# A hybrid attention block: the first unit's key copies and three weight splits in another order

## The chip, the core and the metric

The kernel runs on one core of one Trainium2 chip. The engines are TensorE (PE, matmuls; its weight loads are listed as PEld), VectorE (DVE), ScalarE (ACT), GpSimd (POOL) and SyncE (SP, which here only issues transfers). Each engine has its own instruction stream and works through it in order; across engines the program waits on semaphores. The metric is the device time of one execution in microseconds (us).

## The reference

One decoder block over 16 meta tokens and 512 tokens, width 1024. Eight heads of differential attention and sixteen heads of stick-breaking attention share one input projection; each branch is gated by SiLU and projected, the branches are merged by sigmoid gates, projected out, and added to the residual under a layer norm. Cut to what matters:

```python
proj = jnp.einsum('bld,dn->bln', h, w_in[i])
q_d, k_d, v_d, g_d, q_s, k_s, v_s, g_s, m_d, m_s = jnp.split(proj, IN_OFFSETS, axis=-1)
...
outs_d.append(diff_attn_block(q_d[:, :, :, t0:t1], k_d[:, :, :, :t1], v_d[:, :, :t1],
                              q_pos, slopes, lam))
outs_s.append(stick_breaking_block(q_s[:, :, t0:t1], k_s[:, :, :t1], v_s[:, :, :t1], q_pos))
...
y_d = rms_norm(y_d, diff_subln_g[i]) * (1.0 - lam_init)
br_d = jnp.einsum('blw,wd->bld', y_d * jax.nn.silu(g_d), w_br_diff[i])
br_s = jnp.einsum('blw,wd->bld', y_s * jax.nn.silu(g_s), w_br_sb[i])
merged = jax.nn.sigmoid(m_d + b_gate[i, 0]) * br_d + jax.nn.sigmoid(m_s + b_gate[i, 1]) * br_s
y = jnp.einsum('bld,de->ble', merged, w_out[i])
```

## The kernel before

All values are fp32. A product keeps fp32's accuracy by splitting each operand into a rounded part and a remainder: ACT casts the rounded part (`hi` for weights, L185), DVE subtracts it from the original (`lo`, L190), and PE adds three products, as in L496, L497, L498 (rounded by rounded, rounded by remainder, remainder by rounded).

The work has three stretches. The first, to about 34 us, normalizes and transposes the input. The middle goes through sixteen units, eight differential heads and eight pairs of stick-breaking heads. While PE, ACT and DVE do one unit's attention, the projections of the next unit are woven into it, so that PE always has products to do. The names in one unit: `stage_q` makes the queries `A` (L618 to L621), `stage_k` and later `stage_kv` the keys (`stage_kv` by a scheme of seven products, L697); the keys are staged in `ks` (L703, L704) and stored by transfers on SP's queue into `k0` and `k1`, one tile for each head of the pair (L650, L651). Scores `sc` are matmuls of keys and queries (L761) into two PSUM banks. In a stick-breaking unit ACT reads a score bank twice (L907, L909) and DVE scans it (L913); the weights are transposed on PE (L773) and copied out; the values' products `av` (L922 to L930) are evacuated by ACT (L934, L938), and the next unit's values by ACT L750 and DVE L751. In a differential unit DVE reads the score banks (L841), ACT exponentiates (L845) and DVE combines (L849 to L851). The third stretch, after the units, has eight branch pairs (`pair`, L1055; products L1071, seven steps in three PSUM banks with copies `t` at L1076, L1078, L1080) and the output matmul (L1194), for which `split_out` splits the output weights (ACT L1136, DVE L1137) and lets SP fetch more raw weights. `merged` multiplies and adds the branches (`ss`), `rounded` and `rest` split the sums (`mh` L1116, `ml` L1119).

What sets the order: the first stretch and the third are kept on PE, DVE, ACT and POOL as they are written. There `run` steps through a generator of matmul groups, adds the time that each group states (0.35 in `pair`), and does a listed step as soon as the running time reaches the step's. The middle is written in the same manner, but its order is decided at build by the framework's scheduler, which simulates the engines and places instructions as they become ready in that simulation. So an edit ahead of the middle can change the order of instructions far behind it.

In the first unit the keys come straight from PSUM (`direct` in `stage_k`), one bank for each half of 264 columns. A key tile wants three things of a head's 64 partitions: the rounded part in one half of the partitions, the remainder beside it, and the rounded part again in the other half.

Of the kernel before, what the change touches and what calls it, by code (L numbers as in the profile page):

```python
# [42 lines left out]
LO, HI = slice(0, 64), slice(64, 128)  # L43
# [3 lines left out]
def hybrid_block_kernel(ctx: ExitStack, tc: tile.TileContext, x, meta, emb_g, emb_b, w_in, b_gate,  # L47
                        diff_lambda, subln_g, w_br_d, w_br_s, w_out, ln_g, ln_b, out):
    nc = tc.nc
    v, s, g, pe = nc.vector, nc.scalar, nc.gpsimd, nc.tensor  # L50
# [40 lines left out]
    for n, (kind, i) in enumerate(seq):  # L91
        if kind in ("BD", "BS", "wd", "ws"):
# [6 lines left out]
            o = len(loads)  # L99
# [35 lines left out]
    def fetch(most=99):  # L135

        for order, most in ((sum_loads, 1), (other_loads, most)):
            while order and most:
                l = order[0]
                src, more, tag = loads[l]  # L140
                bufs, log = rings[tag]
                if len(log) >= bufs and left[log[-bufs]] or tag not in pools:
                    break
                raw = pools[tag].tile([P, 4, P], F32, tag=tag, name=tag, bufs=bufs)
                nc.sync.dma_start(raw if l < WOUT else raw.rearrange("p a b -> p (a b)"), src)
                if more is not None:
                    second[l] = [lambda raw=raw, x=x: g.dma_start(raw, x, accum_op=ALU.add) for x in more]  # L147
                    if tag == "rawa":
                        added(l)
                    else:  # L150
                        for n in range(len(more)):
                            later.append((state["n"] + 3 + 3 * n, lambda l=l: added(l)))
                        later.sort(key=lambda x: x[0])
                raws[l] = raw
                log.append(order.pop(0))
                most -= 1
# [220 lines left out]
    def scaled(b, k, eng=s):  # L377

        o, i = hF[k][:, ds(M + P * b, P)], tps[b // 2][k // 2][:, ts(2 * (k % 2) + b % 2, P)]
        if eng is s:  # L380
            s.activation(o, i, AF.Identity, scale=cols[:, k:k + 1], bias=cols[:, 8 + k:9 + k])
        else:
            v.tensor_scalar(o, i, cols[:, k:k + 1], cols[:, 8 + k:9 + k], op0=ALU.mult, op1=ALU.add)

    def query(n, o, w, k):

        pe.matmul(pss[n][:, ds(o, w)], raw0[:, n, k, :], hF[k][:, ds(M + o, w)], start=(k == 0), stop=(k == KT - 1))  # L387
# [3 lines left out]
    def high(half, k, copy):  # L391

        copy(hTh[:, k, HALF[half]], hF[k][:, HALF[half]])
# [55 lines left out]
    def lam2():  # L449
        v.tensor_scalar(nlam, lexp[:, 1:2], lexp[:, 0:1], -LAM_INIT, op0=ALU.subtract, op1=ALU.add)  # L450

    steps = dict(a=scaled, d=lambda b, k: scaled(b, k, v), x=lambda b, k: query(0, P * b, P, k),
                 y=lambda h, k: query(1, 256 * h, 256, k), s=lambda h, k: high(h, k, s.copy),
                 h=lambda h, k: high(h, k, v.tensor_copy), l=low, N=norms, S=stat)
# [48 lines left out]
    def proj_pos(res, kind, i):  # L503
        n = take(kind, i)
        for c in range(2):
            ps = pj.tile([P, 512], F32, tag="pj", name="ps")
            if n > 4:
                prep(n + c + state["ahead"])
            for k in range(KT):
                _, wh, wl = split[n + k // 4]  # L510
                for m, (a, b) in enumerate(((wh, hTh), (wh, hTl), (wl, hTh))):
                    pe.matmul(ps[:, :H2], a[:, k % 4, :], b[:, k, ts(c, H2)], start=(k == 0 and m == 0),  # L512
                              stop=(k == KT - 1 and m == 2))
                if k < KT - 1:
                    yield 0.33
            res.append(ps)
            if c == 0:
                yield 0.33
# [43 lines left out]
    def merge_gate(c, j, t=None):  # L562
        res = []
        yield from proj_tok(res, "m" + "ds"[c], j)
        if t is None:
            t = gpool.tile([P, S], F32, tag="sg", name=f"sm{c}")
        s.activation(t, res[0], AF.Sigmoid, bias=cols[:, 16 + 8 * c + j:17 + 8 * c + j])
        sm[c, j] = t
        yield 0.64

    def run(proj, steps=()):

        steps, now = sorted(steps, key=lambda x: x[0]), 0.0
        for part in proj:
            for dt in part:
                now += dt
                while steps and steps[0][0] <= now:
                    steps.pop(0)[1]()
        for _, step in steps:
            step()  # L580


    with tc.tile_pool(name="att", bufs=1) as ap:
# [18 lines left out]
        K = [ap.tile([P, 2, L], F32R, name=f"k{c}") for c in range(2)]  # L602
# [22 lines left out]
        def stage_k(unit, kind, n, direct=False):  # L625

            pss = []
            proj = proj_pos(pss, "k" + kind, n)
            for m in range(2):
                while len(pss) == m:  # L630
                    yield next(proj, 0.33)
                o, ps = ts(m, H2), pss[m][:, :H2]
                if direct:
                    s.copy(K[0][LO, 0, o], ps[LO])
                    v.tensor_tensor(K[0][LO, 1, o], ps[LO], K[0][LO, 0, o].bitcast(F32), op=ALU.subtract)
                    s.copy(K[0][HI, 0, o], ps[LO])
                    s.copy(K[1][HI, 0, o], ps[HI])
                    v.tensor_tensor(K[1][LO, 1, o], ps[HI], K[1][HI, 0, o].bitcast(F32), op=ALU.subtract)
                    s.copy(K[1][LO, 0, o], ps[HI])  # L639
                    continue  # L640
                t = ap.tile([P, 2, H2], F32R, tag="ks", name="ks", bufs=2)
                s.copy(t[:, 0], ps)
                v.tensor_tensor(t[:, 1], ps, t[:, 0].bitcast(F32), op=ALU.subtract)
                staged.append((o, t))
# [80 lines left out]
        def values(unit, kind):  # L725

            vT = unit["vT"]
            tv = ptp.tile([P, 512], F32, tag="tp", name="tv")
            for j in range(4):
                pe.transpose(tv[:, ts(j, P)], vT[:, ts(j, P)], ident)  # L730
            tvv = tv.rearrange("p (j d) -> p j d", j=4)
            V = ap.tile([P, 1024], F32R, tag="v", name="V")
            t4 = ptp.tile([P, 512], F32, tag="tp", name="t4")[:, :P]
            pe.transpose(t4, strips(vT[:, P:], P), ident)
            if kind == "d":
                V = V.rearrange("p (c j d) -> p c j d", c=2, j=4)
                V = [V[:, c] for c in range(2)]
                s.copy(V[0][:, :3, :], tvv[:, :3, :])
                v.tensor_tensor(V[1][:, :3, :], tvv[:, :3, :], V[0][:, :3, :].bitcast(F32), op=ALU.subtract)
                s.copy(v3[:, 0:2].rearrange("p c d -> p (c d)"), tvv[:, 3, :])  # L740
                h, l = [v4[:, 2 * m:2 * m + 2].rearrange("p c d -> p (c d)") for m in range(2)]
                s.copy(h, t4)
                v.tensor_tensor(l, t4, h.bitcast(F32), op=ALU.subtract)
                unit["V"] = V
            else:

                V = V.rearrange("p (j c d) -> p j c d", j=4, c=4)[:, :3]
                for h, l, src in ((V[:, :, 0:4:3], V[:, :, 1:3], tvv[:, :3].rearrange("p j (c d) -> p j c d", c=2)),
                                  (v4[:, 0:4:3], v4[:, 1:3], t4.rearrange("p (c d) -> p c d", c=2))):
                    s.copy(h, src)  # L750
                    v.tensor_tensor(l, src, h.bitcast(F32), op=ALU.subtract)  # L751
                s.copy(v3[:, 0:3:2], tvv[:, 3].rearrange("p (c d) -> p c d", c=2))
                unit["V"] = [V[:, :, 2 * c:2 * c + 2].rearrange("p j c d -> p j (c d)") for c in range(2)]
# [206 lines left out]
        for u, (kind, n) in enumerate(UNITS):  # L960
# [7 lines left out]
            steps = pending + [(0.6, lambda unit=unit: values(unit, kind))]  # L968
# [163 lines left out]
    def split_out(c, k):  # L1132

        l = WOUT + c * KT + k
        raw = raws[l].rearrange("p a b -> p (a b)")
        s.copy(WO[c][0][:, k, :], raw)  # L1136
        v.tensor_tensor(WO[c][1][:, k, :], raw, WO[c][0][:, k, :].bitcast(F32), op=ALU.subtract)  # L1137
        left[l] -= 1
        fetch()
# [6 lines left out]
    for p in range(4):  # L1146
        steps = []
        if p == 3:
            run([merge_gate(1, 7, MS[7])], [(4.4, further)])
            WO = [[hpool.tile([P, KT, 512], F32R, tag=f"hT{x}", name=f"wo0{x}") for x in "hl"]]  # L1150
            steps = [(0.8 + 1.6 * k, lambda k=k: split_out(0, k)) for k in range(5)]
        run([pair("BS", p, G, MS[2 * p:2 * p + 2], lambda m, p=p: merged(2 * p + m))], steps)


# [29 lines left out]
    for c in range(2):  # L1184
        for t in range(NB):
            st, final = sts[t], t == NB - 1
            for o, w in [(0, 256), (256, 256)] if final and c else [(0, 512)]:
                r, hr = ds(o, w), hrs[t][:, ts(c, 512)]
                ps = pj.tile([P, 512], F32, tag="pj", name="pso")[:, :w]
# [76 lines left out]
```

## Time and profile before

| | |
|---|---|
| median of 3 runs | 707.35 us (707.21 to 707.68) |
| profiled execution | 707.99 us, its span 706.2 us |
| mean granted TensorE clock | 0.997 |
| PE busy | 694.5 us (98% of the span) |
| PE weight loads | 634.7 us (90%) |
| DVE busy | 569.3 us (81%) |
| ACT busy | 440.2 us (62%) |
| POOL busy | 131.4 us (19%) |

The span runs from the first to the last recorded instruction; the execution's own time has 1.8 us around it. A timeline row gives the start and the length of an instruction (with xN, of N in a row), its engine, line, operation, output and input, and in brackets how long the engine stood idle ahead of it and what ended that wait. Matmuls overlap: the next one starts before the modelled end of the one before, so their spacing from start to start tells more than their length.

### The profile page before, as it was taken

To read this page: it belongs to the slowest core of one execution; us is meant where nothing else is said; L and a number is where in the kernel's file an instruction comes from. 1 tells how busy PE (TensorE), PEld (TensorE's weight loads), DVE (VectorE), ACT (ScalarE), POOL (GpSimd) and SP (SyncE) were. 2 spreads that over 40 slices of the span, in tenths; PEclk is the share of its full clock that TensorE was granted. 3 is DMA by queue.
4 is the path that set the end of the run, shared out by engine and by line. 5 is a ranking of instruction groups with operands and counts; after the bars stand their busy time and mean duration, and the time that the engine had idled before them with its cause. 6 is when DMAs were issued, how large, how long until landed. Compare 5 with 4: busy or idle time off the path is not lost.

```text
span 706.2 us, 13286 instructions
## 1 busy us (share of the span) xinstructions
PE 694.5 (98%) x4482; PEld 634.7 (90%) x4482; DVE 569.3 (81%) x1224; ACT 440.2 (62%) x1071; POOL 131.4 (19%) x144
## 2 busy tenths in 40 slices
PE   8999999999999999999999999999999999999995
PEld 8999999989899898998989899987888998999885
DVE  6887998878687787889877898976666788688886
ACT  5776767767566687776768687766555456555400
POOL 3243112223222201212121220000012201230011
PEclk9999999999999999999999999999999999999998
DMA  9399547988888886899898976646575749886702
GB/s 294 97 190 186 145 111 184 210 181 182 218 189 179 203 186 184 169 226 202 207 185 232 189 159 184 172 115 180 197 183 112 157 121 239 153 171 186 270 28 101
DMA packets 184054, 124.93 MB, mean 177 GB/s; under 512 B 8961, under 2 KB 168098, under 8 KB 183986
## 3 DMA queue, kind: packets, MB, share of 16 engines
q1 hardware_dynamic: 147890, 102.84, 50.0%
q0 software_dynamic: 35776, 20.19, 22.9%
q10 hardware_dynamic: 320, 1.06, 0.4%
q8 instruction: 35, 0.57, 0.3%
q14 instruction: 33, 0.27, 0.1%
HBM read 93.54 MB, written 9.44 MB: 146 GB/s over the span
## 4 chain that ended last, share of the span: by engine, by line
PE 92%; DVE 3%; ACT 2%; DMA 2%; issue 1%; POOL 0%; DVEq 0%; SPq 0%; ACTq 0%; POOLq 0%
PE q L697 17%; PE ps L497 11%; PE ps L496 11%; PE ps L498 11%; PE q L1071 11%; PE pso L1194 6%; PE ps L512 6%; PE sc L761 6%; PE t L773 3%; PE bank L387 1%; PE tv L730 1%; PE av L928 1%; PE av L929 1%; DMA k<-ks 1%; DVE w L190 1%
## 5 line engine op out<-in xcount | busy, mean ns | idle before, releaser
L497 PE MATMUL ps<-hTl,w 128*128 128x512 f32 x368 | 144.7, 393 | 0.0
L190 DVE TENSOR_TENSOR w<-raw,w 128x512 fp32r<-128x512 f32 x168 | 114.3, 688 | 37.7 <-ACT w L185 36.4
L498 PE MATMUL ps<-hTh,w 128*128 128x512 f32 x368 | 144.5, 393 | 0.0
L496 PE MATMUL ps<-hTh,w 128*128 128x512 f32 x368 | 144.5, 393 | 0.0
L185 ACT CAST w<-raw 128x512 fp32r<-128x512 f32 x168 | 103.5, 627 | 11.0 <-PE ps L498 4.7
L147 POOL DMA_DIRECT2D rawk<-in_w_in_dram x48 | 66.0, 1628 | 118.9 <-DMA rawk<-in_w_in_dram 53.1
L697 PE MATMUL q<-tS,w 128*128 128x264 f32 x384 | 82.5, 289 | 0.0
L1071 PE MATMUL q<-gh,w 128*128 128x256 f32 x448 | 81.4, 283 | 0.2 <-ACT t L1080 0.2
L498 PEld LDWEIGHTS ps<-hTh,w 128*128 128x128 f32 x368 | 69.2, 188 | 13.4
L497 PEld LDWEIGHTS ps<-hTl,w 128*128 128x128 f32 x368 | 69.2, 188 | 13.2
L496 PEld LDWEIGHTS ps<-hTh,w 128*128 128x128 f32 x368 | 69.2, 188 | 13.0
L1071 PEld LDWEIGHTS q<-gh,w 128*128 128x128 f32 x448 | 70.1, 192 | 0.5 <-ACT t L1080 0.4
L761 PE MATMUL sc<-k,A 128*128 128x264 f32 (+3 forms) x320 | 66.2, 299 | 1.2 <-ACT e L909 0.8
L697 PEld LDWEIGHTS q<-tS,w 128*128 128x128 f32 x384 | 63.6, 188 | 0.3
L1071 PE MATMUL q<-gl,w 128*128 128x256 f32 x224 | 63.4, 283 | 0.0
L697 PE MATMUL q<-hTh,w 128*128 128x264 f32 x288 | 60.8, 286 | 0.0
L913 DVE TENSOR_TENSOR_SCAN e<-e,diag 128x528 f32<-128x528 f32 (+1 forms) x64 | 54.1, 850 | 5.9 <-ACT e L907 5.9
L697 PE MATMUL q<-tl,w 128*128 128x264 f32 x192 | 54.8, 286 | 0.0
L761 PEld LDWEIGHTS sc<-k,A 128*128 128x128 f32 x320 | 49.9, 189 | 3.8 <-ACT e L909 1.2
L512 PE MATMUL ps<-hTh,w 128*128 128x264 f32 x256 | 51.5, 288 | 0.2 <-ACT k L639 0.2
L697 PEld LDWEIGHTS q<-hTh,w 128*128 128x128 f32 x288 | 47.8, 189 | 1.0 <-DVE kvt L717 0.2
L778 ACT CAST ah<-t 128x384 fp32r<-128x384 f32 (+2 forms) x72 | 34.4, 478 | 21.8 <-PE t L773 21.5
(283 smaller groups left out, 1574.0 us busy)
## 6 DMA issues: line engine op xcount, KB each, us to landing
raw<-in_w_in_dram SPq DMA_DIRECT2D x140, 256.0 KB, 3.5
rawk<-in_w_in_dram POOLq DMA_DIRECT2D x48, 256.0 KB, 5.8
rawk<-in_w_in_dram SPq DMA_DIRECT2D x36, 256.0 KB, 3.7
k<-ks SPq DMA_DIRECT2D x60, 132.0 KB, 3.2
raw<-in_w_out_dram SPq DMA_DIRECT2D x16, 256.0 KB, 3.5
k<-ks SPq DMA_DIRECT2D x60, 66.0 KB, 3.2
A<-low SPq DMA_DIRECT2D x28, 128.0 KB, 2.4
raw<-in_w_br_diff_dram SPq DMA_DIRECT2D x12, 256.0 KB, 4.1
```

What stands on the lines that cost most here:

```text
L147: second[l] = [lambda raw=raw, x=x: g.dma_start(raw, x, accum_op=ALU.add) for x in more]
L185: s.copy(wh, raw)
L190: eng.tensor_tensor(wl, raw, wh.bitcast(F32), op=ALU.subtract)
L496: pe.matmul(ps, wh[:, k % 4, :], hTh[:, k, M:], start=(k == 0), stop=False)
L497: pe.matmul(ps, wh[:, k % 4, :], hTl[:, k, M:], start=False, stop=False)
L498: pe.matmul(ps, wl[:, k % 4, :], hTh[:, k, M:], start=False, stop=(k == KT - 1))
L512: pe.matmul(ps[:, :H2], a[:, k % 4, :], b[:, k, ts(c, H2)], start=(k == 0 and m == 0), stop=(k == KT - 1 and m == 2))
L697: pe.matmul(bank, a[:, k, :], b, start=start and k == 0 and j == 0, stop=k == 3 and j == 2, skip_group_check=not start)
L761: pe.matmul(ps[:, :n], q, K[:, m, k0:k0 + n], start=(m == 0), stop=(m == 1))
L913: v.tensor_tensor_scan(rev, rev, diag[0][:, L - nk:][:, ::-1], 0.0, ALU.mult, ALU.max)
L1071: pe.matmul(bank, a[:, k, :], b[:, n, k, :], start=start and k == 0 and m == 0, stop=k == 3 and m == 2, skip_group_check=not start)
L1194: pe.matmul(ps, MH[k][:, ts(t, P)] if m == "h" else ML[:, k, ts(t, P)], WO[c]["hl".index(w)][:, k, r], start=(n == 0), stop=(n == 3 * KT - 1))
```

## The change

Two edits. In `stage_k`, where the keys are taken straight from PSUM, both ACT copies of a head now stand ahead of the DVE subtraction of that head. In the last branch pair, the steps that split the third to the fifth of the output weights' rows are due 0.4 later in `run`'s count.

```diff
                 if direct:
                     s.copy(K[0][LO, 0, o], ps[LO])
+                    s.copy(K[0][HI, 0, o], ps[LO])
                     v.tensor_tensor(K[0][LO, 1, o], ps[LO], K[0][LO, 0, o].bitcast(F32), op=ALU.subtract)
-                    s.copy(K[0][HI, 0, o], ps[LO])
                     s.copy(K[1][HI, 0, o], ps[HI])
+                    s.copy(K[1][LO, 0, o], ps[HI])
                     v.tensor_tensor(K[1][LO, 1, o], ps[HI], K[1][HI, 0, o].bitcast(F32), op=ALU.subtract)
-                    s.copy(K[1][LO, 0, o], ps[HI])
                     continue
...
         if p == 3:
             run([merge_gate(1, 7, MS[7])], [(4.4, further)])
             WO = [[hpool.tile([P, KT, 512], F32R, tag=f"hT{x}", name=f"wo0{x}") for x in "hl"]]
-            steps = [(0.8 + 1.6 * k, lambda k=k: split_out(0, k)) for k in range(5)]
+            steps = [(t, lambda k=k: split_out(0, k)) for k, t in enumerate((0.8, 2.4, 4.4, 6.0, 7.6))]
```

Every engine has the same instructions before and after, in another order. On ACT, the first half of the first keys: before, with what an instruction waits for on other engines,

```order
L634 CAST k0_444<-ps_480 64x264 [waits DMAHW3_49,DMAHW1_49,DMAHW4_49,DMAHW0_49,DMAHW6_49,DVE_49,DMAHW7_49,PE_49,Pool_49]
L636 CAST k0_444<-ps_480 64x264 [waits DVE_49]
L637 CAST k1_445<-ps_480 64x264
L639 CAST k1_445<-ps_480 64x264 [waits DVE_49]
L348 ACTIVATE A0_173<-bank_187 128x512
```

and after:

```order
L634 CAST k0_444<-ps_480 64x264 [waits DMAHW3_49,DMAHW1_49,DMAHW4_49,DMAHW0_49,DMAHW6_49,DVE_49,DMAHW7_49,PE_49,Pool_49]
L635 CAST k0_444<-ps_480 64x264
L637 CAST k1_445<-ps_480 64x264 [waits DVE_49]
L638 CAST k1_445<-ps_480 64x264
L348 ACTIVATE A0_173<-bank_187 128x512
```

The copies stand in the same row; the waits for DVE, two before (ahead of the second and fourth copy), are one now (ahead of the third). The wait that ended ACT's part is on DVE's side: the last subtraction (L639 after) follows the last copy, where before the last copy followed the last subtraction.

On PE, in the stick-breaking unit near 480 us, where `av` are the products of the unit ending, `sc` the scores of the next, `ps` a projection and `t0` the first transposes of the next unit's weights. Before:

```order
L496 MATMUL ps_6607<-hTh_149,w2_6445 128x512
L761 MATMUL sc_6532<-k1_445,A1_5966 128x264
L923 MATMUL av_6400<-af3_6383,v3_432 128x128
...
L930 MATMUL av_6400<-al0_6347,V_6064 128x512
L734 MATMUL t4_6467<-ident_129,sx_6468 128x128
L761 MATMUL sc_6532<-k1_445,A1_5966 128x264
L761 MATMUL sc_6559<-k1_445,A1_5966 128x400 x2
...
L498 MATMUL ps_6607<-hTh_149,w2_6504 128x512
L761 MATMUL sc_6569<-k1_445,A1_5966 128x272 x2
L773 MATMUL t0_6637<-ident_129,apad0_429 128x128 x4
```

After:

```order
L498 MATMUL ps_6607<-hTh_149,w2_6445 128x512
L923 MATMUL av_6400<-af3_6383,v3_432 128x128
...
L930 MATMUL av_6400<-al0_6347,V_6064 128x512
L734 MATMUL t4_6467<-ident_129,sx_6468 128x128
L761 MATMUL sc_6532<-k1_445,A1_5966 128x264 x2
L761 MATMUL sc_6559<-k1_445,A1_5966 128x400 x2
...
L498 MATMUL ps_6607<-hTh_149,w2_6504 128x512
L773 MATMUL t0_6637<-ident_129,apad0_429 128x128 x4
...
L498 MATMUL ps_6607<-hTh_149,w2_6504 128x512
L761 MATMUL sc_6569<-k1_445,A1_5966 128x272 x2
```

The values' row begins four projections and one score matmul sooner, and the scores `sc_6569` stand behind the transposes `t0` and six projections more.

On SP, the stores of the keys between the fourth and the fifth unit, where `ks_1789` and `ks_1868` are the two halves. Before:

```order
L651 DMA k0_444<-ks_1789 64x264
L650 DMA k0_444<-ks_1789 64x2x264
L651 DMA k0_444<-ks_1868 64x264
L651 DMA k1_445<-ks_1868 64x264
L621 DMA A1_1632<-low_1633 64x512
L621 DMA A0_1631<-low_1633 64x512
L650 DMA k0_444<-ks_1868 64x2x264
L650 DMA k1_445<-ks_1789 64x2x264
```

After:

```order
L651 DMA k0_444<-ks_1789 64x264
L651 DMA k1_445<-ks_1789 64x264
L621 DMA A1_1632<-low_1633 64x512
L621 DMA A0_1631<-low_1633 64x512
L650 DMA k0_444<-ks_1789 64x2x264
L650 DMA k1_445<-ks_1789 64x2x264
L650 DMA k0_444<-ks_1868 64x2x264
L651 DMA k0_444<-ks_1868 64x264
```

The store of the first half's two parts (L650) stands behind both `A` stores now, and directly ahead of the second half's.

On ACT in the last branch pair, where `wo0h` are the output weights and `t` the pair's copy; before and after:

```order
L1116 CAST mh_8420<-ss_7672 128x512
L1136 CAST wo0h_8366<-raw_8269 128x512
L1080 COPY t_8371<-q_8368 128x256
L1136 CAST wo0h_8366<-raw_8314 128x512
L1136 CAST wo0h_8366<-raw_8376 128x512
```

```order
L1116 CAST mh_8420<-ss_7672 128x512
L1080 COPY t_8371<-q_8368 128x256
L1136 CAST wo0h_8366<-raw_8269 128x512
L1136 CAST wo0h_8366<-raw_8314 128x512
L1136 CAST wo0h_8366<-raw_8376 128x512
```

The copy changes places with one cast. On DVE the subtraction of that cast (L1137) goes behind the second `ml` (L1119) in the same way.

## The prediction, on record before the changed kernel ran

> **What bounds the kernel now.** I read the page first, for busy shares; then the waits of TensorE (PE); then busy time by stretches; and last the timelines around each wait. The page's rows:
>
> ```profile
> span 706.2 us, 13286 instructions
> PE 694.5 (98%) x4482; PEld 634.7 (90%) x4482; DVE 569.3 (81%) x1224; ACT 440.2 (62%) x1071; POOL 131.4 (19%) x144
> ```
>
> PE is busy for 694.5 of 706.2 us. No matmul is added, removed or resized by this change, so only PE's idle time can move. Where that idle time lies from the first keys on, first by what ended it, then by stretch (second pair of numbers: PE busy, instructions):
>
> ```profile
> PE sc L761 <- ACT e L909: 0.8, 1, 0.8
> PE sc L761 <- DMA k<-ks: 0.4, 1, 0.4
> PE ps L512 <- ACT k L639: 0.2, 1, 0.2
> ```
>
> ```profile
> 34.00:385.00 351.00, 351.00 (x2360) 325.55 (x2359) 291.40 (x706) 248.18 (x642) 78.94 (x74) 1.00 0.83 188
> 385.00:404.00 19.00, 18.59 (x111) 16.29 (x110) 15.46 (x30) 12.74 (x33) 4.84 (x4) 1.00 0.95 205
> ...
> 478.00:484.00 6.00, 5.19 (x30) 4.29 (x29) 2.01 (x4) 3.56 (x11) 0.81 (x1) 1.00 0.60 177
> 484.00:644.00 160.00, 160.00 (x1002) 144.93 (x1001) 121.19 (x228) 85.35 (x164) 26.09 (x22) 1.00 0.72 169
> 644.00:650.00 6.00, 5.81 (x48) 5.60 (x47) 4.38 (x7) 5.38 (x12) 0.00 (x0) 1.00 0.61 165
> ```
>
> From 34 to 650 us PE stands still for 0.41 + 0.81 + 0.19 = 1.4 us by these rows, and the granted clock is 1.00 throughout. Ahead of the first keys the order is unchanged. A modelled matmul end hides part of a stall, so I size each from start to start, against the spacing of its neighbours. That gives, as shown below, 0.4 at the first keys, 0.57 at 403, 0.97 at 483, 0.35 at 649.8 and 0.1 at 658: 2.4 us in all, 0.34% of the time. **That is the ceiling of any gain.** A loss has no ceiling, since the change re-orders the middle of the program, where PE has no slack.
>
> **The change, part by part.** *The first unit's keys.* Two halves of 264 columns, each with four copies (ACT) and two subtractions (DVE) from one PSUM tile; counts and shapes stay. The first half:
>
> ```profile
> 30.95 0.37 ACT L634 CAST k<-ps 64x264 fp32r<-64x264 f32 x1 [3.04 <-DVE nlam L450]
> ...
> 31.82 0.37 ACT L636 CAST k<-ps 64x264 fp32r<-64x264 f32 x1 [0.49 <-DVE k L635]
> 32.21 0.38 ACT L637 CAST k<-ps 64x264 fp32r<-64x264 f32 x1
> 33.09 0.38 ACT L639 CAST k<-ps 64x264 fp32r<-64x264 f32 x1 [0.50 <-DVE k L638]
> ```
>
> ```profile
> 31.36 0.42 DVE L635 TENSOR_TENSOR k<-ps,k 64x264 fp32r<-64x264 f32 x1
> ...
> 32.62 0.43 DVE L638 TENSOR_TENSOR k<-ps,k 64x264 fp32r<-64x264 f32 x1 [0.84 <-ACT k L637]
> ```
>
> ```profile
> 33.52 0.39 PE L512 MATMUL ps<-hTh,w 128*128 128x264 f32 x1 [0.22 <-ACT k L639]
> ```
>
> Before, the chain is copy, subtract, two copies, subtract, copy: four hand-overs between ACT and DVE, and the matmul that reuses the bank starts at 33.52. After, it is two copies, subtract, two copies, subtract: three. Two copies side by side cost 0.39 (31.82 to 32.21); a copy to the subtraction behind it takes 0.41 (30.95 to 31.36, 32.21 to 32.62); a subtraction to the copy behind it 0.46 (31.36 to 31.82, 32.62 to 33.09). So the copies start at 30.95 and 31.34, the subtraction at 31.75, copies at 32.21 and 32.60, the subtraction at 33.01, and PE follows 0.43 after a last copy's start, some 0.48 after a subtraction that is 0.05 longer: 33.49. **Gain 0.03**, bounds −0.05 and +0.1 by the scatter of those links: the hand-over that goes is paid back by the copy that now stands ahead of the first subtraction.
>
> The Trainium skill, "PSUM — Partial Sum Buffer", section "PSUM bank collisions raise a hardware error", says two engines collide only in the same bank and the same 32 partitions, reads included. By that rule the second head's copies, which read partitions 64 to 127, need not wait for the first head's subtraction, and an order that used it could take 0.4 off; the wait of 0.49 above is between readers of the same partitions and agrees, but the changed program still lets the second head's first copy wait for DVE, so nothing of it is gained here.
>
> The second half has the same six instructions and lies under matmuls that do not wait (no idle in 34 to 385): nothing. If that cover went, it would count as the first half does.
>
> *The middle, 85 to 486 us.* The source does not change there, but the build's scheduler decides that order anew. Two stalls lie in it. The larger:
>
> ```profile
> 480.97 0.58 ACT L934 COPY half<-av 64x512 f32<-64x512 f32 x1 [2.41 <-issue]
> ...
> 482.98 0.41 ACT L909 ACTIVATE e<-sc 128x264 f32<-128x264 f32 x1
> ```
>
> ```profile
> 482.02 0.39 PE L497 MATMUL ps<-hTl,w 128*128 128x512 f32 x1
> 482.25 0.39 PE L498 MATMUL ps<-hTh,w 128*128 128x512 f32 x1
> 483.45 0.52 PE L761 MATMUL sc<-k,A 128*128 128x272 f32 x2 [0.81 <-ACT e L909]
> ```
>
> ACT idles 2.41 until the attention values' last matmul, then runs six in a row; the last frees the score bank. PE has 1.20 from 482.25 to 483.45 where the matmul before took 0.23: 0.97 lost. In the new order the values' matmuls stand five earlier (four of 0.23, one of 0.12: 1.0 us), so ACT starts near 480.0 and, with one smaller copy more in its row (at most 0.4, as L909), frees the bank between 482.4 and 482.8 where it was 483.4. The score matmul moves behind four transposes and six projections, 1.4 us for the latter alone: from 482.5, where it stood but for the stall, to 483.9 or later. Slack on both sides: **gain 0.9** (0.5 to 0.97). Late next are the transposes that now stand ahead: they need the last result of
>
> ```profile
> 482.68 0.56 DVE L751 TENSOR_TENSOR V<-tv,V 128x384 fp32r<-128x384 f32 x1 [3.39 <-ACT V L750]
> 483.16 0.28 DVE L751 TENSOR_TENSOR v<-t,v 128x128 fp32r<-128x128 f32 x1
> ```
>
> which moves 1.0 earlier with ACT, its second part to 482.2, with 0.28 of work: ready at 482.4 to 482.5, just as PE arrives. That is the lower bound of 0.5.
>
> The smaller one, on a stored key:
>
> ```profile
> 398.85 1.28 SPq L650 DMA_DIRECT2D k<-ks  x2
> ```
>
> ```profile
> 402.42 0.40 PE L761 MATMUL sc<-k,A 128*128 128x264 f32 x2
> 403.23 0.48 PE L761 MATMUL sc<-k,A 128*128 128x264 f32 x2 [0.41 <-DMA k<-ks]
> ```
>
> PE took 0.81 from the one row to the other for two matmuls at 0.12 (the spacing of rows of this width, see 649.33 below): 0.57 lost. The store was issued at 398.85, 4.38 before the matmul. After, the value matmuls of that unit stand some 3 us earlier, which lifts a wait from DVE ahead of the key's sums; but a DVE step that waits for a GpSimd transfer moves ahead of them too, and SP, which issues in order and is the last to come (its issues stand 0.6 apart), has one `A` store more in front. I take the store 0.2 earlier: **gain 0.2**, from −0.4 (one SP issue later) to 0.57.
>
> The Trainium skill, "DMA: Bandwidth & Descriptors", section "Anatomy of one DMA — SWDGE (gpsimd) path", gives about 2.0 us plus bytes over 436 GB/s. By that a store of 132 KB would land in an estimated 2.3 us, and there would be no stall at 403 to regain, the sum being smaller by 0.2; the row's 4.38 decides against it.
>
> *The last branch pair.* ACT's copy of t now stands ahead of one cast of output weights:
>
> ```profile
> 649.38 0.37 ACT L1080 COPY t<-q 128x256 f32<-128x256 f32 x1
> ...
> 656.48 1.66 ACT L1136 CAST wo0h<-raw 128x512 fp32r<-128x512 f32 x3
> ```
>
> ```profile
> 649.21 0.28 PE L1071 MATMUL q<-gl,w 128*128 128x256 f32 x1
> 649.33 0.28 PE L1071 MATMUL q<-gh,w 128*128 128x256 f32 x1
> 649.80 0.38 PE L1071 MATMUL q<-gh,w 128*128 128x256 f32 x1 [0.19 <-ACT t L1080]
> ...
> 657.87 0.39 PE L1194 MATMUL pso<-wo0h,ml 128*128 128x512 f32 x1
> 658.19 0.50 PE L1194 MATMUL pso<-wo0h,mh 128*128 128x512 f32 x1
> ```
>
> The spacing is 0.12, the step to 649.80 is 0.47: 0.35 lost. ACT is in a row without idle there, so the copy starts one cast earlier, about 0.5 (three take 1.66), and the stall goes whole. But it comes back: at 658.19 the output matmul (0.32 after the one before it, 0.1 over the 0.23 of that width) needs the last of the three casts that begin at 656.48, and these follow DVE's merges. DVE works back to back from 648 to 656, the one step of it that waits for that cast (0.1) now standing one later, so the casts come 0.1 earlier at most while PE would come 0.35 earlier. The rest turns up as a longer wait at 658. **Gain 0.1**, bounds 0 and 0.35. The loads that SP issues behind the three moved splits go out by the same 0.5 later:
>
> ```profile
> raw<-in_w_out_dram SPq DMA_DIRECT2D x16, 256.0 KB, 3.5
> ```
>
> At 3.5 us each they land some 3 us ahead of the casts at 656.48, so I count them at nothing.
>
> *New waits elsewhere.* Every place of the middle is permuted by up to 37 PE, 14 DVE, 12 ACT and 9 SP rows. Before, it hides all but two stalls (rows above); after, I allow 0.2 for small ones, with 0 and 1.5 as bounds, the upper end being the two middle stalls of before once more.
>
> **Sum:** −0.03 − 0.9 − 0.2 − 0.1 + 0.2 = −1.0 us. The profiled execution took 707.99 us (span 706.2 and 1.8 around it) and would take 707.0; it stands 0.64 over the median of the runs, 707.35, which I carry over: **706.4 us**. A difference under 0.2%, 1.4 us, is about what a measurement of this kernel cannot tell from no change.
>
> **The rivals.** *Faster by over 0.2%:* all five stalls go and no new one comes: 2.4 us, 705.0. For it: they are single and small, and a reshuffle with no matmul added can only lose by waits. Against it: the 658 wait takes back 0.25, and 403 is set by SP, whose new order is not shorter. It is reached from 1.4 us, so 403 must go whole beside 483. Chance 0.27.
>
> *The reorder gives nothing:* the transposes at 483 wait for V as the score matmul did, SP is one issue later at 403, and 658 takes all: 0.5 gained, 0.4 lost, 707.2. It ends within 0.2% too; chance 0.2. That part one does nothing by itself is part of every case.
>
> *Slower:* the key stores between the fourth and fifth unit.
>
> ```profile
> 122.82 0.43 DVE L704 TENSOR_TENSOR ks<-kvt,ks 128x264 fp32r<-128x264 f32 x1
> ...
> 126.29 0.41 DVE L704 TENSOR_TENSOR ks<-q,ks 128x264 fp32r<-128x264 f32 x1
> ```
>
> ```profile
> 128.09 1.33 SPq L650 DMA_DIRECT2D k<-ks  x2
> ```
>
> ```profile
> 132.36 0.41 PE L761 MATMUL sc<-k,A 128*128 128x264 f32 x2
> ```
>
> ```profile
> k<-ks SPq DMA_DIRECT2D x60, 132.0 KB, 3.2
> ```
>
> Before, the first key's sum is done at 122.82 and SP spreads its stores; after, it stands next to the second's, near 126.3 to 126.9, and six stores leave in one row. The one that releases the score matmul (128.09 before) goes out third and fourth, near 128.3 and 128.9, and PE asks 0.9 later, near 133.3. With the median 3.2 us it lands at 132.1, with the 4.38 of 403 at 133.3. So it decides when that issue comes after 128.9 to 130.1. To end over 0.2% slower, 1.4 + 1.0 = 2.4 us of stall are needed, four more SP issues of 0.6: 708.8 or more. Against it: DVE would have to be 2 us late in a stretch that never stopped PE. Chance, with other such places, 0.12.
>
> By the Trainium skill's formula named above that store would land in an estimated 2.3 us, and this rival would fall to half its chance; the two rows of 3.2 and 4.38 say otherwise.
>
> **How the numbers follow.** My forecast, 706.4 with its own range of 705.9 to 707.0, has 0.41; with the case of nothing gained (0.2) that makes 0.61 within 0.2%, 0.27 faster, 0.12 slower. The range goes from 705.1 (all stalls but the 0.1 that 658 keeps) to 708.2 (the allowance for new waits at its upper end, 1.5, the gain at 483 at its lower bound, 403 at nothing): about a tenth is left out on each side.
>
> **What the changed profile would show.** The wait of the score matmul on ACT's L909 gone near 482, and the transposes in its place with under 0.4; the wait on the stored key near 402 shorter or gone; the matmul at 33.5 unmoved within 0.1; no wait on L1080, but the wait of the output matmul on the third cast up from 0.1 to 0.35. The matmul count and busy time of PE unchanged. It would be wrong if PE shows a wait on a stored key near 133, or on a value or weight between 85 and 486 where it had none, of more than a microsecond; or if 403 goes whole, which would put it near 705.6.

## The result, and the profile after

The changed kernel takes 709.45 us (median of 6 runs, 709.21 to 709.87 but for one of 711.45), the kernel before 707.51 beside it: ratio 1.0032 (95% interval 1.0022 to 1.0042). It is slower by about 1.9 us, where I had forecast 1.0 us less and a range that ended at 708.2. In two executions, one of run 1 below and one of the kernel before beside runs 1 to 4, the granted clock fell to 0.85 and 0.77; they took 761.0 and 843.1 us and are left out of the ratios.

The page, the waits of PE and its busy time by stretches, the same views as of the kernel before (profiled execution 709.38 us):

```profile
span 707.6 us, 13275 instructions
PE 695.4 (98%) x4482; PEld 634.9 (90%) x4482; DVE 570.6 (81%) x1224; ACT 443.5 (63%) x1071; POOL 131.2 (19%) x144
```

```profile
PE sc L761 <- DMA k<-ks: 1.9, 1, 1.9
...
PE ps L512 <- DVE k L639: 0.3, 1, 0.3
PE pso L1194 <- ACT wo0h L1136: 0.3, 1, 0.3
```

```profile
34.00:300.00 266.00, 265.82 (x1796) 246.94 (x1796) 218.93 (x565) 188.16 (x477) 62.59 (x60) 1.00 0.82 181
300.00:350.00 50.00, 48.14 (x320) 44.25 (x320) 42.76 (x82) 36.16 (x97) 9.23 (x8) 1.00 0.89 211
350.00:478.00 128.00, 128.00 (x807) 115.66 (x806) 108.13 (x207) 91.08 (x237) 18.76 (x17) 1.00 0.77 179
478.00:484.00 6.00, 6.00 (x36) 5.34 (x36) 2.11 (x5) 3.47 (x9) 0.00 (x0) 1.00 0.33 97
...
644.00:650.00 6.00, 6.00 (x45) 5.69 (x43) 5.02 (x9) 4.84 (x10) 0.86 (x1) 1.00 0.82 177
```

The waits at 403, 483 and 649.8 are gone, as forecast (the same work stands later here; the place of 649.8 falls behind 650, and the list of waits shows none on L1080). But in 300 to 350, where PE had no idle time before, it now stands still for 1.9 us, at one place, for a stored key:

```profile
338.90 0.28 PE L697 MATMUL q<-hTh,w 128*128 128x264 f32 x1
341.04 0.48 PE L761 MATMUL sc<-k,A 128*128 128x264 f32 x2 [1.86 <-DMA k<-ks]
```

From start to start, against the 0.12 of its neighbours, that is 2.02 us lost. The store behind it (in the program this matmul waits for the L650 store of the second half into `k0`), and the rows of SP and DVE that lead up to it; first the kernel before (the store is the third SP row, the subtraction whose result it stores the DVE row), then the changed one (the store is the first of the last SP row):

```profile
322.01 0.97 SPq L145 DMA_DIRECT2D raw<-in_w_in_dram  x2
328.15 0.34 SPq L530 DMA_DIRECT2D gs<-ys  x1
...
330.95 0.94 SPq L650 DMA_DIRECT2D k<-ks  x1
```

```profile
329.32 0.41 DVE L704 TENSOR_TENSOR ks<-q,ks 128x264 fp32r<-128x264 f32 x1
```

```profile
327.04 0.37 SPq L145 DMA_DIRECT2D raw<-in_w_in_dram  x1
328.26 0.34 SPq L530 DMA_DIRECT2D gs<-ys  x1
329.74 0.37 SPq L145 DMA_DIRECT2D raw<-in_w_in_dram  x1
330.20 1.36 SPq L651 DMA_DIRECT2D k<-ks  x1
...
335.08 0.54 SPq L621 DMA_DIRECT2D A<-A  x1
337.38 1.29 SPq L650 DMA_DIRECT2D k<-ks  x2
```

```profile
334.03 0.43 DVE L704 TENSOR_TENSOR ks<-q,ks 128x264 fp32r<-128x264 f32 x1
```

```profile
SPq L650 <- DMA raw<-in_w_in_dram: 1.7, 1, 1.7
```

Three things are late at once. The subtraction (L704) went from 329.32 to 334.03. The store was issued 6.4 us later (330.95 to 337.38), and 1.7 us of that SP waits for a weight load: in the program SP's transfers take eight completion semaphores in turn (DMAHW0 to DMAHW7), and an issue waits until the transfer eight places ahead of it, the last on its semaphore, has landed; that is the load of 329.74. And the two weight loads (L145) themselves stand at 327.04 and 329.74 instead of 322.01 and 322.61: behind three accumulating loads of GpSimd (324.5 to 326.0) and not ahead of them. Ahead of them they landed after 2.9 and 3.0 us, behind them the first took 6.4. Of the transfers issued from 329 to 335.5 (KB each, median us to landing), before and after:

```profile
k<-ks SPq DMA_DIRECT2D x3, 66.0 KB, 4.7
```

```profile
k<-ks SPq DMA_DIRECT2D x3, 66.0 KB, 6.4
```

Why the loads are late stands on ACT and DVE: they wait for raw buffers that DVE's subtractions for two weights (L190) free, and these follow ACT's casts (L185). ACT before (one row of two) and after:

```profile
320.61 1.14 ACT L185 CAST w<-raw 128x512 fp32r<-128x512 f32 x2 [0.97 <-PE q L697]
```

```profile
322.44 0.58 ACT L934 COPY half<-av 64x512 f32<-64x512 f32 x1 [1.39 <-issue]
...
324.94 0.64 ACT L185 CAST w<-raw 128x512 fp32r<-128x512 f32 x1
...
326.23 0.66 ACT L185 CAST w<-raw 128x512 fp32r<-128x512 f32 x1
```

DVE before and after:

```profile
321.30 1.28 DVE L190 TENSOR_TENSOR w<-raw,w 128x512 fp32r<-128x512 f32 x2
```

```profile
326.34 0.67 DVE L190 TENSOR_TENSOR w<-raw,w 128x512 fp32r<-128x512 f32 x1
...
329.05 0.67 DVE L190 TENSOR_TENSOR w<-raw,w 128x512 fp32r<-128x512 f32 x1
```

In the new order the values' evacuation (L934) has moved ahead of the casts on ACT, and on DVE the second subtraction starts 2.2 us behind the end of its cast (326.89 to 329.05), with other steps in front. This last link is read from the trace; it was not tried by itself.

### The profile page after: what moved, and what is told of

It is laid out like the page before. It is cut to its first block, busy times and chain, and to the rows that moved or that the text cites. A ratio compares the mean times of both kernels' runs of the same rounds, so it can differ in the third digit from the quotient of the medians.

```text
span 707.6 us, 13275 instructions
## 1 busy us (share of the span) xinstructions
PE 695.4 (98%) x4482; PEld 634.9 (90%) x4482; DVE 570.6 (81%) x1224; ACT 443.5 (63%) x1071; POOL 131.2 (19%) x144
## 4 chain that ended last, share of the span: by engine, by line
PE 91%; DVE 5%; DMA 1%; issue 1%; ACT 1%; DVEq 0%; SPq 0%; POOL 0%; ACTq 0%
PE q L697 17%; PE ps L497 11%; PE ps L498 11%; PE ps L496 11%; PE q L1071 10%; PE ps L512 6%; PE pso L1194 6%; PE sc L761 6%; PE t L773 4%; PE bank L387 1%; PE tv L730 1%; DMA xt<-in_x_dram 1%; PE av L928 1%; PE av L929 1%; DVE w L190 1%
## 5 line engine op out<-in xcount | busy, mean ns | idle before, releaser
L190 DVE TENSOR_TENSOR w<-raw,w 128x512 fp32r<-128x512 f32 x168 | 114.2, 686 | 37.2 <-ACT w L185 36.5
L185 ACT CAST w<-raw 128x512 fp32r<-128x512 f32 x168 | 103.6, 627 | 14.2 <-PE ps L498 4.7
L697 PE MATMUL q<-hTh,w 128*128 128x264 f32 x288 | 64.6, 291 | 0.0
L939 POOL DMA_DIRECT2D ys<-half x14 | 11.7, 838 | 196.4 <-ACT ys L938 93.7
```

What stands on the lines that cost most here:

```text
L185: s.copy(wh, raw)
L190: eng.tensor_tensor(wl, raw, wh.bitcast(F32), op=ALU.subtract)
L697: pe.matmul(bank, a[:, k, :], b, start=start and k == 0 and j == 0, stop=k == 3 and j == 2, skip_group_check=not start)
```

## The experiments

Where a kernel has the order of one stretch or engine changed, a table of given orders holds every engine in the named order; nothing else differs.

**1. The first edit alone** (keys; weight splits as before):

```diff
-            steps = [(t, lambda k=k: split_out(0, k)) for k, t in enumerate((0.8, 2.4, 4.4, 6.0, 7.6))]
+            steps = [(0.8 + 1.6 * k, lambda k=k: split_out(0, k)) for k in range(5)]
```

> The first edit alone (order of the first unit's key copies), the weight splits as before; the middle then stands in the order of the changed kernel. Theory 1 (the loss is the re-ordered middle, above all one late key store at 341 us): about 709.5 us, +2.0 against before, with the 1.9 us wait of the score matmul on the stored key near 341. Rival 2 (the later weight splits cost the time at the output matmul): 707.5, same as before. Rival 3 (the copies themselves are slower at 33 us): slower too, but by a later matmul at 33.5 of one microsecond or more.

Measured: 709.71 against 707.36, ratio 1.0033 (1.0022 to 1.0044). In its profile the same matmul waits, 1.40 us from start to start:

```profile
339.92 0.48 PE L761 MATMUL sc<-k,A 128*128 128x264 f32 x2 [1.24 <-ACT e L909]
```

The profile names ACT here, which had long been done; SP waits for the weight load ahead of the store in this run too (1.2 us). The profiled execution took 708.36, five others 709.26 to 710.45, so the loss varies from one execution to the next. The first edit carries the whole loss.

**2. The second edit alone:**

```diff
-            steps = [(0.8 + 1.6 * k, lambda k=k: split_out(0, k)) for k in range(5)]
+            steps = [(t, lambda k=k: split_out(0, k)) for k, t in enumerate((0.8, 2.4, 4.4, 6.0, 7.6))]
```

> The second edit alone (three weight splits later), keys and middle as before. Theory 1: 707.4, within 0.2 us of before: the wait on the copy t at 649.8 gone (0.35), the wait of the output matmul on the third cast up by about as much less 0.1. Rival 2: about 709.5. Rival 3: 707.5.

Measured: 707.35 against 707.36, ratio 0.9999 (0.9991 to 1.0008). The wait on t is gone and its like stands at the output matmul:

```profile
PE pso L1194 <- ACT wo0h L1136: 0.2, 1, 0.2
```

0.42 more than its neighbours from start to start there (0.09 before): 0.35 gained, 0.33 given back. Rival 2 is out.

**3. Both edits, the middle in the order of before** (given for every engine).

> Both edits, but a table holds the middle on every engine in the order that it has in the kernel before. Theory 1: 707.4, no wait on a stored key at 341, the waits at 403 (0.57) and 483 (0.97) of before back. Rival 2 or 3 (an edit costs by itself): 709.0 to 709.6.

Measured: 707.29, ratio 1.0001 (0.9992 to 1.001). The edits cost nothing by themselves; rivals 2 and 3 are out. The wait at 483 is back (0.97); the one at 403 was in neither profile of runs 2 and 3, so in the old order it comes and goes.

**4. The changed kernel with one stretch, 318 to 342 us, as before:**

> The changed kernel, with the order of before on every engine in one stretch only, 318 to 342 us. Theory 1 (one place): 707.4, 2.0 us less than the changed kernel; the wait at 341 gone and nothing else moved. Rival 4 (the loss is spread over the re-ordered middle in many small waits): 708.5 to 709.4.

Measured: 707.18, ratio 0.9999 (0.999 to 1.0008).

```profile
300.00:350.00 50.00, 50.00 (x339) 46.28 (x337) 44.23 (x84) 36.82 (x99) 9.22 (x8) 1.00 0.88 210
```

PE does not stand still there, and some 2.3 us against the changed kernel are back. Rival 4 is out: the loss is made in these 24 us. What is left of the new order comes out about even with the kernel before (707.18 against 707.36): in this profile the wait at 483 (0.97) is gone, and 0.58 at 256 and 0.28 at 132 are new.

**5. The kernel before with that one stretch in the new order:**

> The kernel before with one stretch, 318 to 342 us, in the order of the changed kernel on every engine; both edits absent. If that stretch is enough for the loss: 709.2 to 709.6, with a wait on the stored key of about 2 us near 341 and the wait at 483 (0.97) kept. If it needs what stands elsewhere in the new middle (SP or DVE arriving late from before 318): 707.4 to 708.5.

Measured: 708.78 against 707.47, ratio 1.0021 (1.0012 to 1.0031); the wait on the stored key is there:

```profile
340.09 0.48 PE L761 MATMUL sc<-k,A 128*128 128x264 f32 x2 [1.83 <-DMA k<-ks]
```

(this execution took 711.31, the slowest of ten.) The stretch alone makes 1.3 us of loss, 0.4 under the lower end of my figure; the new order ahead of it may make the rest, which was not tried.

**6. The stores first on SP.** SP's rows near 334 in the changed kernel, and here:

```
 DMA k_444<-ks_4603 (L651)              DMA k_444<-ks_4603 (L651)
 DMA gd (L556)                          DMA k_445<-ks_4603 (L651)
 DMA k_445<-ks_4603 (L651)              DMA k_444<-ks_4603 (L650)
 DMA A_4694<-A_4693 (L621)              DMA k_445<-ks_4603 (L650)
 DMA k_444<-ks_4603 (L650)              DMA gd (L556)
 DMA k_445<-ks_4603 (L650)              DMA A_4694<-A_4693 (L621)
```

> The changed kernel; on SP alone, near 334 us, the two stores of the second half's keys (L650) go ahead of the gate store (L556) and of the query store (L621). Three theories of the late store. S (it is issued late, because SP waits until the weight load issued eight transfers earlier has landed, 337.3): it goes out at 334.6 right behind its subtraction and lands 3.3 later, the wait is gone, 707.4. B (backlog: every transfer issued from 329 to 335 took 5.5 to 7.4 us): it lands near 339.9 as its neighbour issued at 334.5 did, 0.9 of the 2.0 us wait stays, 708.3. D (the subtraction on DVE is late, at 334.03): it can leave no earlier than 334.5, so as S or B.

Measured: 708.40, ratio 1.0015 (1.0006 to 1.0025).

```profile
340.27 0.48 PE L761 MATMUL sc<-k,A 128*128 128x264 f32 x2 [1.14 <-DMA k<-ks]
```

```profile
SPq L556 <- DMA raw<-in_w_in_dram: 1.9, 1, 1.9
```

The stores leave at 334.96, 2.4 us sooner, and the gate store now does the waiting for the load. Yet 1.30 of 2.02 us stay, since the store takes 5.2 us and lands only at 340.1. That is B with S for the smaller part: of the loss, the late issue is 0.7 us by these profiles and 1.05 by the medians.

**7. The subtraction early on DVE:** L704 of `ks_4603` moved from behind L914 to behind L555, four rows up.

> The changed kernel; on DVE alone the subtraction of the second half's keys (L704, 334.03) goes ahead of four rows, to about 332.6. D (late subtraction): the wait at 341 falls by 1.4 or more, 708.0 or less. S and B: SP stands at its wait for the weight load as before, nothing changes, 709.4.

Measured: 710.12, ratio 1.0033 (1.0022 to 1.0043).

```profile
341.78 0.48 PE L761 MATMUL sc<-k,A 128*128 128x264 f32 x2 [2.79 <-DMA k<-ks]
```

```profile
SPq L650 <- DMA raw<-in_w_in_dram: 2.3, 1, 2.3
```

No gain, though the subtraction started at 332.34 and not at 334.03: SP stands at the load, not at the subtraction. D by itself is out; this run gives back 1.7 of the 4.7 us by which the subtraction is late, so it does not show what the order of before, with the subtraction at 329.32, would do on SP.

**8. The weight load later on SP:** the L145 row of 329.74 moved behind both L650.

> The changed kernel; on SP alone the weight load issued at 329.7 goes behind the two key stores (about 336.5). The store now waits, eight transfers back, for a gate store that had landed at 334.5, and 256 KB less stand ahead of it. S and B together: it is issued near 335.7 and lands near 339.0 to 339.5, the wait at 341 falls to 0.5 or less, 707.4 to 707.9. S with the backlog unchanged (its length set by GpSimd's loads alone): it lands near 341, as its neighbour issued at 335.1 did at 340.5, and 1.5 of 2.0 stay: 708.9. If the load itself is needed soon, a wait on a weight appears instead, after 345.

Measured: 708.74, ratio 1.0017 (1.0008 to 1.0027).

```profile
340.56 0.48 PE L761 MATMUL sc<-k,A 128*128 128x264 f32 x2 [1.21 <-DMA k<-ks]
```

I expected 0.5 or less and got 1.37 from start to start: the issue is 2.1 us sooner (335.25), but 256 KB less ahead of it did not shorten the backlog, in which GpSimd's last load landed at 337.0 as in the changed kernel. A miss of mine in size; the forecast with an unchanged backlog is the nearer one.

**9. A quarter of the bytes in GpSimd's three loads:**

```diff
-                    second[l] = [lambda raw=raw, x=x: g.dma_start(raw, x, accum_op=ALU.add) for x in more]
+                    second[l] = [lambda raw=raw, x=x: (state.update(a=state.get("a", -1) + 1), g.dma_start(*((y[:, :1] if state["a"] in (35, 36, 37) else y) for y in (raw, x)), accum_op=ALU.add)) for x in more]
```

`state["a"]` counts these loads; 35 to 37 are the three of 324.5 to 326.0.

> The changed kernel, same order; the three accumulating weight loads that GpSimd issues between 324.5 and 326.0 move a quarter of their bytes each (64 of 256 KB; the other three quarters of three sums are left out, so the output is not the reference's). B (the stores wait in a backlog that these loads make with two weight loads of SP): transfers issued from 329 to 335 take 3 to 4 us in place of 5.5 to 7.4, the weight load lands before SP needs its semaphore, the key store is issued near 335.7 and lands near 339.0; the wait at 341 falls to 0.3 or less, 707.5. If the backlog is made by SP's own transfers: the wait stays at 1.3 to 2.0, 708.7 to 709.4.

Measured: 707.03 against 707.40, ratio 0.9993 (0.9984 to 1.0003). Same order as the changed kernel, and the wait is gone:

```profile
338.98 0.40 PE L761 MATMUL sc<-k,A 128*128 128x264 f32 x2
```

```profile
k<-ks SPq DMA_DIRECT2D x3, 66.0 KB, 3.2
```

A store takes 3.2 us in place of 6.4, and SP issues L650 at 334.61. The backlog of GpSimd's loads with SP's late ones makes the larger part of the loss, and the wait for the semaphore too. These three loads are not what the change brought in: the kernel before has them at the same time (324.4 to 325.9), with its store issued at 330.95 and no wait. They are what a late store runs into. The Trainium skill, "DMA: Bandwidth & Descriptors", section "Queues, rings and completion order", says that each DMA engine takes turns between queues, and that a semaphore's increment lands only after every earlier write of that engine, across its queues. The run agrees as far as both queues share the engines: shorter loads on GpSimd's queue halved the landing time on SP's. Which of the two rules does it, the run does not tell.

**10. The kernel before with the two weight loads as late:** on SP, the two L145 of 322.01 moved behind L530.

> The kernel before, where on SP alone the two weight loads issued at 322.0 and 322.6 go behind the gate store of 328.2, as late as the changed kernel has them. B: GpSimd's three loads land sooner (by about 331), and the key stores issued from 329 to 334 take 5 us or more where they took 2.4 to 5.0; PE asks for the first of them at 339.0, so the time stays at 707.4 to 708.0. If the two loads don't matter: landing times as in the kernel before. If the wait eight transfers back decides by itself: SP holds a store until a load has landed, near 335, and a wait of up to 1 us appears at 341.

Measured: 707.75, ratio 1.0007 (0.9998 to 1.0016); no wait at 341 (the one at 403 was 0.82). The small stores took 4.8 us where they took 4.7, the larger 3.6 against 2.7, and GpSimd's loads landed no sooner (334.9 for the last, 333.8 before), so my reading of them was wrong. Late loads alone are not enough: here the store into `k0` still left at 332.6, 4.8 us ahead of the changed kernel's. Which of the other changes in the stretch must come to them, the order of SP or that of DVE, was not taken apart.

**11. The kernel before with two stretches of the new order, 383 to 411 and 476 to 487:**

> The kernel before (both edits absent), with the changed kernel's order on every engine in two stretches, 383 to 411 and 476 to 487 us. The theory that the re-order gains at 403 and 483 what the prediction said, and loses at 341 alone: the wait at 483 gone (0.97), the one at 403 gone where it occurs (0 to 0.57, two profiles of the old middle had none), 706.2 to 706.5, faster than both kernels.

Measured: 710.88, ratio 1.0041 (1.0028 to 1.0054), the worst of all. 483 is without a wait, but

```profile
405.56 0.48 PE L761 MATMUL sc<-k,A 128*128 128x264 f32 x2 [2.17 <-DMA k<-ks]
```

A miss: the new order at 403 is not better in itself. The picture is that of 341, with SP's key stores issued at 402.31 (398.85 before) behind two weight loads and GpSimd's three. The changed kernel has no wait there, though its store leaves just as late (402.30), since PE comes to the key only at 406.09, and here at 402.99. Run 4, with the new order there but not in 318 to 342, has none either (store at 400.17, PE at 403.94). Which part of the order ahead of 383 makes the store late against PE in this run was not tried.

**12. The kernel before with one stretch of the new order, 476 to 487:**

> As the run with two stretches, but with the changed kernel's order from 476 to 487 us alone. The wait at 483 gone, the one at 403 as before: 706.4 to 706.6.

Measured: 706.40 against 707.40, ratio 0.9988 (0.9979 to 0.9997): faster than both kernels. The wait at 483 is gone, and this profile has none at 403 either.

```profile
478.00:484.00 6.00, 6.00 (x35) 5.09 (x35) 3.52 (x6) 4.59 (x13) 0.81 (x1) 1.00 0.65 176
```

## Why the prediction was wrong, point by point

The ceiling was sound: 2.4 us of waits, and no run was faster than by 1.0. What failed is the term for new waits in the middle, which I set at 0.2 with 1.5 as its bound: it measured 2.76, of which 2.02 at one place, the stored key at 341. The bound was taken from the two stalls of before, not from any place of the new order. By start-to-start times in the two profiles:

| term | predicted | measured |
|---|---|---|
| first keys | −0.03 | +0.06 |
| wait at 483 | −0.9 | −0.97 |
| wait at 403 | −0.2 | −0.57 |
| last pair: 649.8 and 658 | −0.1 | −0.35 + 0.33 |
| new: stored key at 341 | | +2.02 |
| new: 256 | | +0.58 |
| new: stored key at 132 | | +0.16 |
| new waits together | +0.2 | +2.76 |

That makes +1.26; with 0.19 ahead of the first keys, where nothing changed, it is the 1.4 between the spans (706.2 and 707.6). The medians are 1.9 apart: the loss varies, and the profiled execution before was 0.5 over its median. Its wait of 0.57 at 403 has that size and is in none of the profiles of runs 2, 3 and 12, which have the old order there. So the median from which I took off 0.2 for 403 may not have held that wait at all; this is a reading and was not tried.

*First keys.* The order came as worked out, but its last link was mis-sized. After:

```profile
32.78 0.38 ACT L638 CAST k<-ps 64x264 fp32r<-64x264 f32 x1
```

```profile
33.19 0.43 DVE L639 TENSOR_TENSOR k<-ps,k 64x264 fp32r<-64x264 f32 x1 [0.83 <-ACT k L638]
```

```profile
33.77 0.36 PE L512 MATMUL ps<-hTh,w 128*128 128x264 f32 x1 [0.28 <-DVE k L639]
```

PE followed the subtraction's start by 0.58, where I took 0.48, and the copy by 0.43 before. With a loss of 0.06 it lies 0.01 outside my bounds, and run 3 shows that it does not count.

*483* was right in mechanism and size, and run 12 shows it alone: 1.0 us. *The last pair* was right step by step, the give-back a little larger than I had it.

*403* came out at its bound in the changed kernel, by luck. I took the store 0.2 earlier; it left 3.45 later, at 402.30 and not at 398.85. PE was later still, held up at 341 among other places, and came to this key at 406.09 (before: 402.42), when the store had landed. The two rows after:

```profile
402.30 1.28 SPq L650 DMA_DIRECT2D k<-ks  x2
```

```profile
406.09 0.65 PE L761 MATMUL sc<-k,A 128*128 128x264 f32 x4
```

In the old order runs 2, 3 and 12 have no wait there and run 10 has one of 0.82; in the new order run 11 has one of 2.33. I had no ground to call it a gain of the order.

*The slower rival* was the right mechanism at the wrong place: a key's subtraction late on DVE, SP's stores bunched behind it, PE waiting. At 132, where I put it, the wait was 0.16 (0.57 in run 8's profile), about inside its margin as I had worked out; the same pattern at the boundary near 330 was one I did not cost. I had gone by where the order put the subtraction and the store, and not by what the moved weight loads meet. The step that failed is the issue, not the latency: at 341 the store landed within 3.7 us (issued at 337.38, PE at 341.04), inside my 3.2 to 4.38, but SP could not issue it sooner, and for 1.7 us it stood at one of the moved loads. An earlier issue would not have kept that latency either: in run 6 it was 5.2. My argument against this rival, that DVE would have to be 2 us late, left out that SP can be held by a load. The chance of 0.12 rested on one place that I had costed, while every boundary between two units has key stores of this kind.

The 2.3 us for such a store, by which this rival would have had half its chance, is worked out from a fit that the Trainium skill ("DMA: Bandwidth & Descriptors", section "Anatomy of one DMA — SWDGE (gpsimd) path") gives for transfers that GpSimd issues. These stores are issued by SP; of the 60 of L650 in the changed kernel the quickest took 2.4 us and the median one 3.3.

*256* is a small one, and no stored key:

```profile
255.66 0.28 PE L697 MATMUL q<-tS,w 128*128 128x264 f32 x1
256.09 0.47 PE L882 MATMUL ms<-sqh,onesm 128*128 128x512 f32 x1
256.59 0.39 PE L697 MATMUL q<-hTh,w 128*128 128x264 f32 x1
```

It is in every profile that has the new order there (runs 1, 4 and 6 to 9 besides) and in none that has the old. The profile puts its second half down to ACT's copy of `gr` (L538) and names nothing for the first; its cause was not followed up.

## What to carry to other kernels

When a scheduler decides the order, an edit of a few instructions can cost more far behind it than at its own place: hold the rest in its old order and look at the edit alone (run 3), then put back the new order one stretch at a time (runs 4, 5 and 12), which here also found a faster kernel than either. Where PE has no slack, follow each store or load that it waits for through its queue: what is ahead of it there, on other queues too, bears on when it lands, and the transfer that last used its semaphore can hold back its issue.

## What the runs showed of the hardware that I had not expected

Stores of 66 KB took 3.2 us (the median of three) with GpSimd's three accumulating loads at a quarter of their size and 6.4 us with them whole, though they are on another queue. At the first keys PE followed a DVE instruction's start by 0.58 us (after, and run 3) and an ACT instruction's by 0.43 (before, and run 2), of 0.43 and 0.38 us length: with the lengths taken off, the hand-over to PE was 0.15 from DVE and 0.05 from ACT.
